# Phase tables in four operations, final states added once, and the layer norm of v on ScalarE and GpSimd

## The chip, the cores and the metric

The kernel runs on one core of a Trainium2 chip. The metric is the device time of one execution in microseconds (us). Before the change three executions took 1104.30, 1105.35 and 1107.51 us (median 1105.35). One more was profiled: it took 1104.05 us, and its span, from the first to the last instruction, is 1102.3 us.

## The reference

One decoder layer on 1024 prompt tokens and 64 sample tokens (8 sequences of 8), model width 1024, all in 32-bit floats:

```python
p = rmsnorm(x, norm1) @ w_in                       # 512 columns for S5, 512 u, 512 v
o_s5, hr, hi = s5_mixer(p[:, :512], h0, ...)       # 32 groups, 64 complex states each
u, v = gelu(p[:, 512:1024]), layernorm(gelu(p[:, 1024:]), ln_g, ln_b)
o_cm = u * (tril(W_s) @ v + b_s)                   # 8 heads, chunks of 128 positions
x = x + concat(rmsnorm(o_s5), rmsnorm(o_cm)) @ w_out
x = x + swiglu(rmsnorm(x), w_gate, w_up, w_down)
y = rmsnorm(x)
```

The S5 recurrence is `h[t] = a h[t-1] + B u[t]` with a complex diagonal `a`. The final states `hr`, `hi` and the rows of the normalised v in the last chunk are outputs too.

## The kernel before

**Stages.** The first is the norm and the S5 columns of the input projection (quarters 0 and 1 of `w_in`, `s5_in`, three token chunks of 384, 384 and 320). The second, from about 75 to 225 us, runs two things side by side: the S5 scan in eight parts of four groups (`s5_a`, `s5_b`, `s5_c`), and the gMLP branch: quarters 2 and 3 of the weights for v (`v_quarter`, nine blocks `j` of 128 tokens), the layer norm of each block (`ln`), then quarters 4 and 5 for u and the mixing (`cm_out`, a chunk at a time). Third comes the gated unit of S5 (`glu`), which reads all of the scan's output, then the output projection, and from about 360 us the feed-forward part, which fills two thirds of the span. Every large matmul is done three times (`mm3`, lines 150 to 152), for the high and low halves of its operands.

**Order.** The framework orders the instructions of each engine by a simulated timeline: it takes what is ready by its own costs, with the order of the code as the priority. Each engine then runs its list strictly in order, and so does the queue of transfers on SyncE (SP). The code of the S5 scan stands ahead of that of the gMLP branch; between them is no other order.

**Phase tables.** The scan is done in a rotating frame: 64 steps of cos and sin per group, split into a coarse and a fine table of eight entries, `tca, tsa` and `tcb, tsb`, made by doubling (lines 431 to 449: three levels each, six VectorE operations a level). For each part `s5_a` multiplies them out into `CO` and `SI` by six VectorE operations on 256 elements (lines 537 to 542), and ScalarE mirrors them (544) and copies the last column (545). `e64` holds that column.

**Final states.** `s5_a` computes the chunk sums by four matmuls in two PSUM banks, ScalarE copies 272 columns of each to `Ss` (510), and VectorE adds the last eight of each group to `fs` (511). Two transfers then swap the halves of `Ss` (513, 514).

**Layer norm of v.** `v_quarter(3, j)` ends with a GELU by ScalarE (650); `ln(j)` is then VectorE's statistics (654, 655), the addition of EPS (656), GpSimd's power of -0.5 (657), and the scaling on VectorE (658). Mixing (680) and the two outputs made on GpSimd (710, 711) read the result.

**Weights.** `load_q` brings half a quarter (512 KB) into a tile called `raw`, and ScalarE and VectorE split it into `cwr` (lines 146 and 147). There are three `raw` tiles for the whole kernel. Besides weights they hold masks and the two outputs of v. In the code the loads for quarter 4 (707) follow all of `ln`, and those for quarter 5 (715) follow the outputs of v.

Of the kernel before, what the change touches and what calls it, by code (L numbers as in the profile page):

```python
# [10 lines left out]
F32 = mybir.dt.float32  # L11
F32R = mybir.dt.float32r
I32 = mybir.dt.int32
AF = mybir.ActivationFunctionType
ALU = mybir.AluOpType
# [5 lines left out]
W = 512  # L21
NG = 32
# [6 lines left out]
EPS = 1e-6  # L29
# [54 lines left out]
def layer_kernel(ctx: ExitStack, tc: tile.TileContext, A, O, dbg=None):  # L84
# [133 lines left out]
    def pt(name, shape):  # L218
        return prep.tile([128] + list(shape), F32, tag=name, name=name)
# [111 lines left out]
    with tc.issue_after(GATE[GA].ins):  # L331
# [80 lines left out]
        fs = s5p.tile([128, NG, 9], F32, name="fs")  # L412
        t4, t5 = pt("e1", [NG, 8]), pt("t5", [NG])
# [11 lines left out]
        V.tensor_scalar(sn[:, 3:10, :], sn[:, 3:10, :], nsgn, None, op0=ALU.mult)  # L425

        e64 = s5p.tile([128, 2, NG], F32, name="e64")
        V.tensor_copy(e64[:, 0, :], co[:, 9, :])
        V.tensor_copy(e64[:, 1, :], sn[:, 9, :])
        tabs = {}  # L430
        for nm, lv, j0 in (("b", 3, 3), ("a", 3, 6)):
            n = 1 << lv
            tcn = s5p.tile([128, NG, n], F32, name=f"tc{nm}")
            tsn = s5p.tile([128, NG, n], F32, name=f"ts{nm}")
            V.memset(tcn[:, :, 0:1], 1.0)
            V.memset(tsn[:, :, 0:1], 0.0)
            for l in range(lv):
                m = 1 << l
                ec = co[:, j0 + l, :].unsqueeze(2).to_broadcast([128, NG, m])
                es = sn[:, j0 + l, :].unsqueeze(2).to_broadcast([128, NG, m])  # L440
                w1, w2 = pt("x1", [NG, 4])[:, :, :m], pt("e2", [NG, 4])[:, :, :m]
                V.tensor_tensor(w1, tcn[:, :, 0:m], ec, ALU.mult)
                V.tensor_tensor(w2, tsn[:, :, 0:m], es, ALU.mult)
                V.tensor_tensor(tcn[:, :, m:2 * m], w1, w2, ALU.subtract)
                w3, w4 = pt("e3", [NG, 4])[:, :, :m], pt("e4", [NG, 4])[:, :, :m]
                V.tensor_tensor(w3, tsn[:, :, 0:m], ec, ALU.mult)
                V.tensor_tensor(w4, tcn[:, :, 0:m], es, ALU.mult)
                V.tensor_tensor(tsn[:, :, m:2 * m], w3, w4, ALU.add)
            tabs[nm] = (tcn, tsn)
# [13 lines left out]
    BUFS = {"U": 2, "bc": 2, "T": 2, "Q": 2, "S": 2, "W": 2, "C": 2, "I": 2, "H": 2}  # L463
# [10 lines left out]
    def s5_a(pi):  # L474
# [31 lines left out]
        for h in range(2):  # L506
            sb = bank("sb", "s5")
            for g in range(2):
                PE.matmul(sb[:, 136 * g:136 * g + 136], Pg[:, 2 * h + g, :], U[:, 2 * h + g, :], start=True, stop=True)
            S.activation(Ss[:, 2 * h:2 * h + 2, :].rearrange("p g c -> p (g c)"), sb[:, 0:272], AF.Copy)  # L510
        V.tensor_tensor(fs[:, gs, 1:9], fs[:, gs, 1:9], Ss[:, :, 128:136], ALU.add)
# [14 lines left out]
        CO, SI = wt("C", "CO", (4, 128)), wt("I", "SI", (4, 128))  # L526
        t = wt("T2", "ct", (4, 8, 8))
        (tca, tsa), (tcb, tsb) = tabs["a"], tabs["b"]
        ch, sh = (x[:, :, 63:127].rearrange("p g (a b) -> p g a b", a=8) for x in (CO, SI))

        def oa(x):
            return x[:, gs, :].unsqueeze(3).to_broadcast([128, 4, 8, 8])

        def ob(x):
            return x[:, gs, :].unsqueeze(2).to_broadcast([128, 4, 8, 8])

        V.tensor_tensor(ch, oa(tca), ob(tcb), ALU.mult)
        V.tensor_tensor(t, oa(tsa), ob(tsb), ALU.mult)
        V.tensor_tensor(ch, ch, t, ALU.subtract)
        V.tensor_tensor(sh, oa(tsa), ob(tcb), ALU.mult)  # L540
        V.tensor_tensor(t, oa(tca), ob(tsb), ALU.mult)
        V.tensor_tensor(sh, sh, t, ALU.add)
        for i, x in enumerate((CO, SI)):
            S.activation(x[:, :, 0:63], x[:, :, 126:63:-1], AF.Copy, scale=(1.0, -1.0)[i])
            S.activation(x[:, :, 127:128], e64[:, i, gs].unsqueeze(2), AF.Copy)
# [46 lines left out]
    for pi in range(8):  # L592
        s5_b(pi)
        if pi < 7:
            s5_a(pi + 1)
        s5_c(pi)
    Q.dma_start(O["fs"], fs)
# [44 lines left out]
    st = lncp.tile([128, 9, 6], F32, name="st")  # L642
    mv = lncp.tile([128, 9, 2], F32, name="mv")

    def v_quarter(q, j):
        p = bank("pv")
        for k in range(8):
            wh, wl = wq(q, k, slice(0, 256))
            mm3(p[:, 0:256], xh[:, k, tok(j)], xl[:, k, tok(j)], wh, wl, k == 0, k == 7)
        S.activation(v[:, j, 256 * (q - 2):256 * (q - 1)], p[:, 0:256], AF.Gelu_apprx_tanh, scale=r1c[:, j:j + 1])  # L650

    def ln(j):
        vj = v[:, j, :]
        V.bn_stats(st[:, j, :], vj)
        V.bn_aggr(mv[:, j, :], st[:, j, :])
        V.tensor_scalar(mv[:, j, 1:2], mv[:, j, 1:2], EPS, None, op0=ALU.add)
        P.tensor_tensor(mv[:, j, 1:2], mv[:, j, 1:2], mhalf[:, 0:1], ALU.pow)
        V.tensor_scalar(vj, vj, mv[:, j, 0:1], mv[:, j, 1:2], op0=ALU.subtract, op1=ALU.mult)
# [165 lines left out]
    i = 0  # L824
# [515 lines left out]
```

## Time and profile before

| | |
|---|---|
| three executions, median | 1105.35 us |
| profiled execution, its time and its span | 1104.05 us, 1102.3 us |
| TensorE busy | 1049.9 us, 95% |
| VectorE busy | 852.9 us, 77% |
| ScalarE busy | 434.3 us, 39% |
| GpSimd busy | 320.5 us, 29% |
| mean granted clock of TensorE | 0.985 |

PE is TensorE (PEld its weight loads), DVE VectorE, ACT ScalarE, POOL GpSimd, and SPq the queue of transfers. A busy share is that of the whole span; what a stage is bound by shows in the windows of that stage, and in what each engine waited for. Durations of neighbouring instructions overlap by some tenths of a us, so the cost of one more in a full queue is the distance of two starts, a little less than its duration.

### The profile page before, as it was taken

The numbers are of one execution on the slowest core, as the hardware profiler recorded it, in microseconds if no ns is written. First come the engines' busy times: TensorE is split into PE (matmuls) and PEld (weight loads), VectorE is DVE, ScalarE is ACT, GpSimd is POOL, SyncE is SP. The second block draws the span as 40 slices with busy tenths as digits, with TensorE's granted clock in tenths as the row PEclk, the third lists the DMA queues.
The fourth block names the chain that finished last, engine by engine and source line by source line (L and its number), as shares of the span: only waits on it lengthen the run. The fifth ranks groups of instructions, "written<-read, shape, count | busy, mean of one in ns | idle before, by whom it ended". The sixth has DMA issues, their size and how long they took to land.

```text
span 1102.3 us, 20323 instructions
## 1 busy us (share of the span) xinstructions
PE 1049.9 (95%) x7966; PEld 1026.8 (93%) x7966; DVE 852.9 (77%) x1724; ACT 434.3 (39%) x812; POOL 320.5 (29%) x287
## 2 busy tenths in 40 slices
PE   7899999979999799999999999999998999999994
PEld 6899998879999699999999999999998999999994
DVE  6987999999998996666666666657668768758886
ACT  7314333487544543233233232233244325314651
POOL 5010350000000435425435334435433333223220
PEclk9989999989999899999999999999999999999998
DMA  8342334375332113223224223133156816514304
GB/s 278 108 129 65 89 99 124 90 225 164 113 113 95 39 58 129 77 90 129 75 76 137 82 77 128 59 110 127 61 181 219 303 40 205 184 35 151 119 16 162
DMA packets 81520, 131.19 MB, mean 119 GB/s; under 512 B 8977, under 2 KB 60049, under 8 KB 81297
## 3 DMA queue, kind: packets, MB, share of 16 engines
q1 hardware_dynamic: 81424, 129.91, 36.3%
q8 instruction: 62, 1.02, 0.4%
q14 instruction: 34, 0.27, 0.1%
HBM read 90.43 MB, written 34.24 MB: 113 GB/s over the span
## 4 chain that ended last, share of the span: by engine, by line
PE 50%; DVE 7%; DMA 5%; issue 2%; ACT 1%; POOL 0%; DVEq 0%; ACTq 0%; POOLq 0%; SPq 0%
PE u L152 12%; PE u L150 12%; PE u L151 12%; DMA h<-hid_d 4%; PE ua L152 3%; PE ua L151 2%; PE ua L150 2%; PE ub L151 1%; PE ub L152 1%; DVE xl L147 1%; PE ub L150 1%; ACT xh L146 1%; DVE fb L147 1%; PE uc L151 1%; PE uc L152 1%
## 5 line engine op out<-in xcount | busy, mean ns | idle before, releaser
L1059 POOL TENSOR_TENSOR tS<-q,q 128x512 f32<-128x512 f32 x22 | 28.6, 1301 | 251.7 <-DVE h L921 146.1
L150 PE MATMUL u<-xh,h 128*128 128x272 f32 x344 | 99.1, 288 | 0.0
L151 PE MATMUL u<-xl,h 128*128 128x272 f32 x344 | 99.0, 288 | 0.0
L152 PE MATMUL u<-xh,h 128*128 128x272 f32 x344 | 98.9, 288 | 0.0
L146 ACT ACTIVATE h<-q 128x512 fp32r<-128x512 f32 (+1 forms) x83 | 50.7, 614 | 81.7 <-PE u L151 56.8
L147 DVE TENSOR_TENSOR h<-q,h 128x512 fp32r<-128x512 f32 (+1 forms) x83 | 72.6, 876 | 4.3 <-ACT h L146 2.5
L150 PE MATMUL pu<-xh,cwr 128*128 128x384 f32 (+1 forms) x192 | 65.5, 345 | 6.2 <-DVE us L303 6.2
L1097 ACT ACTIVATE st<-st 128x272 f32<-128x272 f32 x88 | 37.8, 431 | 72.0 <-DVE st L1119 34.8
L152 PE MATMUL pu<-xh,cwr 128*128 128x384 f32 (+1 forms) x192 | 65.1, 342 | 0.0
L151 PEld LDWEIGHTS u<-xl,h 128*128 128x128 f32 x344 | 64.9, 189 | 0.0
L151 PE MATMUL pu<-xl,cwr 128*128 128x384 f32 (+1 forms) x192 | 64.8, 338 | 0.0
L150 PEld LDWEIGHTS u<-xh,h 128*128 128x128 f32 x344 | 64.7, 188 | 0.0
L152 PEld LDWEIGHTS u<-xh,h 128*128 128x128 f32 x344 | 64.6, 188 | 0.0
L1064 POOL TENSOR_TENSOR tS<-tS,q 128x512 f32<-128x512 f32 x22 | 30.0, 1363 | 111.3 <-DVE h L147 59.6
L146 ACT ACTIVATE fb<-q 128x512 fp32r<-128x512 f32 (+1 forms) x64 | 38.9, 609 | 58.3 <-PE u L151 35.8
L152 PE MATMUL u<-xh,fb 128*128 128x272 f32 x208 | 61.1, 294 | 0.6 <-DVE fb L147 0.6
L150 PE MATMUL u<-xh,fb 128*128 128x272 f32 x208 | 60.6, 291 | 0.1
L151 PE MATMUL u<-xl,fb 128*128 128x272 f32 x208 | 60.5, 291 | 0.0
L147 DVE TENSOR_TENSOR fb<-q,fb 128x512 fp32r<-128x512 f32 (+1 forms) x63 | 53.4, 850 | 5.3 <-ACT fb L146 4.4
L152 PE MATMUL po<-xh,cwr 128*128 128x272 f32 x192 | 55.9, 291 | 0.0
L151 PE MATMUL po<-xl,cwr 128*128 128x272 f32 x192 | 55.8, 290 | 0.0
L150 PE MATMUL po<-xh,cwr 128*128 128x272 f32 x192 | 55.5, 289 | 0.0
(498 smaller groups left out, 4122.8 us busy)
## 6 DMA issues: line engine op xcount, KB each, us to landing
hid_d<-st SPq DMA_DIRECT2D x22, 952.0 KB, 4.2
h<-hid_d SPq DMA_DIRECT2D x28, 544.0 KB, 4.0
q<-in_w_gate_dram SPq DMA_DIRECT2D x22, 512.0 KB, 3.5
q<-in_w_up_dram SPq DMA_DIRECT2D x22, 512.0 KB, 3.5
q<-in_w_d_dram SPq DMA_DIRECT2D x16, 512.0 KB, 3.7
wo<-in_w_out_dram SPq DMA_DIRECT2D x14, 512.0 KB, 4.9
wi<-in_w_in_dram SPq DMA_DIRECT2D x12, 512.0 KB, 5.1
h<-hid_d SPq DMA_DIRECT2D x14, 408.0 KB, 3.1
```

The costliest lines, as they stand in the source:

```text
L146: S.activation(hi, src, AF.Copy)
L147: return (eng or V).tensor_tensor(lo, src, hi.bitcast(F32), ALU.subtract)
L150: PE.matmul(p, wh, ah, start=start, stop=False, **kw)
L151: PE.matmul(p, wh, al, start=False, stop=False, **kw)
L152: return PE.matmul(p, wl, ah, start=False, stop=stop, **kw)
L1059: P.tensor_tensor(tS, a21, a22, ALU.add)
L1064: P.tensor_tensor(tS, tS, a11, ALU.subtract)
L1097: S.activation(dst, src, AF.Silu)
```

## The change

The fine table gets four entries at half steps (two levels in place of three, from the entries of `sn` and `co` one octave lower), the coarse one eight as before, started from the fine one's last entry. The tables are stored as pairs, so that sum and difference of two products give the forward and the backward half of each row: four VectorE operations a part. ScalarE makes the swapped copies once. The last eight columns are copied by ScalarE from PSUM to a tile `fsb`, and one addition after the last part puts them into `fs`. The layer norm takes its sum from the accumulator of the GELU, the sum of squares from a ScalarE pass that writes to a `raw` tile, five GpSimd operations on one column, and a ScalarE pass for the scaling.

```diff
-        V.tensor_scalar(sn[:, 3:10, :], sn[:, 3:10, :], nsgn, None, op0=ALU.mult)
+        V.tensor_scalar(sn[:, 2:10, :], sn[:, 2:10, :], nsgn, None, op0=ALU.mult)
...
+        tcb, tsb = (s5p.tile([128, NG, 2, 4], F32, name=n) for n in ("tcb", "tsb"))
+        ta1, ta2 = (s5p.tile([128, NG, 2, 8], F32, name=n) for n in ("ta1", "ta2"))
+        def powers(cs, ss, lv, j0):
...
+        V.tensor_copy(tcb[:, :, 0, 0], co[:, 2, :])
+        V.tensor_copy(tsb[:, :, 0, 0], sn[:, 2, :])
+        powers(tcb[:, :, 0, :], tsb[:, :, 0, :], 2, 3)
+        V.tensor_copy(ta1[:, :, 0, 0], tcb[:, :, 0, 3])
+        V.tensor_copy(ta1[:, :, 1, 0], tsb[:, :, 0, 3])
+        powers(ta1[:, :, 0, :], ta1[:, :, 1, :], 3, 6)
+        for x in (tcb, tsb):
+            S.activation(x[:, :, 1, :], x[:, :, 0, :], AF.Copy)
+        S.activation(ta2[:, :, 0, :], ta1[:, :, 1, :], AF.Copy)
+        S.activation(ta2[:, :, 1, :], ta1[:, :, 0, :], AF.Copy, scale=-1.0)
...
-            S.activation(Ss[:, 2 * h:2 * h + 2, :].rearrange("p g c -> p (g c)"), sb[:, 0:272], AF.Copy)
-        V.tensor_tensor(fs[:, gs, 1:9], fs[:, gs, 1:9], Ss[:, :, 128:136], ALU.add)
+            sb = sb[:, 0:272].rearrange("p (g c) -> p g c", g=2)
+            S.activation(Ss[:, 2 * h:2 * h + 2, 0:128], sb[:, :, 0:128], AF.Copy)
+            S.activation(fsb[:, g0 + 2 * h:g0 + 2 * h + 2, :], sb[:, :, 128:136], AF.Copy)
...
-        V.tensor_tensor(ch, oa(tca), ob(tcb), ALU.mult)
-        V.tensor_tensor(t, oa(tsa), ob(tsb), ALU.mult)
-        V.tensor_tensor(ch, ch, t, ALU.subtract)
-        V.tensor_tensor(sh, oa(tsa), ob(tcb), ALU.mult)
-        V.tensor_tensor(t, oa(tca), ob(tsb), ALU.mult)
-        V.tensor_tensor(sh, sh, t, ALU.add)
+        V.tensor_tensor(t1, oa(ta1), ob(tcb), ALU.mult)
+        V.tensor_tensor(t2, oa(ta2), ob(tsb), ALU.mult)
+        V.tensor_tensor(body[:, :, :, 4:8], t1, t2, ALU.subtract)
+        V.tensor_tensor(body[:, :, :, 3::-1], t1, t2, ALU.add)
         for i, x in enumerate((CO, SI)):
             S.activation(x[:, :, 0:63], x[:, :, 126:63:-1], AF.Copy, scale=(1.0, -1.0)[i])
-            S.activation(x[:, :, 127:128], e64[:, i, gs].unsqueeze(2), AF.Copy)
+        S.activation(CS[:, :, :, 127], e64[:, gs, :], AF.Copy)
...
+    V.tensor_tensor(fs[:, :, 1:9], fs[:, :, 1:9], fsb, ALU.add)
     Q.dma_start(O["fs"], fs)
...
-        S.activation(v[:, j, 256 * (q - 2):256 * (q - 1)], p[:, 0:256], AF.Gelu_apprx_tanh, scale=r1c[:, j:j + 1])
+        S.activation(v[:, j, 256 * (q - 2):256 * (q - 1)], p[:, 0:256], AF.Gelu_apprx_tanh, scale=r1c[:, j:j + 1],
+                     accum_out=st[:, j, q - 2:q - 1])
...
     def ln(j):
         vj = v[:, j, :]
-        V.bn_stats(st[:, j, :], vj)
-        V.bn_aggr(mv[:, j, :], st[:, j, :])
-        V.tensor_scalar(mv[:, j, 1:2], mv[:, j, 1:2], EPS, None, op0=ALU.add)
+        P.tensor_tensor(mv[:, j, 0:1], st[:, j, 0:1], st[:, j, 1:2], ALU.add)
+        P.tensor_scalar(mv[:, j, 0:1], mv[:, j, 0:1], -1.0 / W, None, op0=ALU.mult)
+        sq = raw("sqv", (W,))
+        S.activation(sq, vj, AF.Square, bias=mv[:, j, 0:1], accum_out=st[:, j, 2:3])
+        P.tensor_scalar(mv[:, j, 1:2], st[:, j, 2:3], 1.0 / W, EPS, op0=ALU.mult, op1=ALU.add)
         P.tensor_tensor(mv[:, j, 1:2], mv[:, j, 1:2], mhalf[:, 0:1], ALU.pow)
-        V.tensor_scalar(vj, vj, mv[:, j, 0:1], mv[:, j, 1:2], op0=ALU.subtract, op1=ALU.mult)
+        P.tensor_scalar(mv[:, j, 0:1], mv[:, j, 0:1], mv[:, j, 1:2], None, op0=ALU.mult)
+        S.activation(vj, vj, AF.Identity, scale=mv[:, j, 1:2], bias=mv[:, j, 0:1])
```

## Rows read from the trace of the kernel before

**Rows 1.** A wait of PE: engine, line, releaser, us in total, times, longest.
```profile
PE pu L150 <- DVE us L303: 6.2, 2, 5.2
```
**Rows 2.** Windows: us, then busy PE, PEld, DVE, ACT, POOL, granted clock, DMA share, GB/s.
```profile
55.50:61.50 6.00, 5.94 (x19) 5.97 (x20) 6.00 (x32) 0.00 (x0) 0.00 (x0) 0.50 0.00 1
110.00:155.00 45.00, 45.00 (x347) 43.35 (x346) 44.29 (x108) 15.52 (x36) 17.72 (x15) 1.00 0.31 84
75.00:225.00 150.00, 148.21 (x1141) 137.26 (x1139) 138.09 (x314) 57.77 (x130) 27.98 (x29) 1.00 0.37 101
231.10:235.40 4.30, 4.30 (x13) 4.30 (x14) 4.30 (x13) 4.30 (x14) 0.00 (x0) 0.50 1.13 361
```
**Rows 3.** Timeline around the first gated matmul; line 586: min/median/max ns, first and last start.
```profile
223.63 0.40 ACT L587 ACTIVATE ys<-yb 128x272 f32<-128x272 f32 x1 [0.29 <-PE yb L586]
224.51 4.10 SPq L757 DMA_DIRECT2D g<-ys_d  x4
231.10 2.61 PE L150 MATMUL pg<-xh,wgh 128*128 128x384 f32 x7 [6.01 <-ACT xh L770]
L586 PE MATMUL yb<-Hp,QK x64: 277/279/383, 111.3 to 223.3; 128*128 128x136 f32 x64
```
**Rows 4.** Timeline of DVE inside PE's wait at 50 us, first and last of six.
```profile
50.60 0.28 DVE L442 TENSOR_TENSOR x<-tcb,co 128x128 f32<-128x128 f32 x1
52.72 0.28 DVE L448 TENSOR_TENSOR tsb<-e,e 128x128 f32<-128x128 f32 x1
```
**Rows 5.** DVE by line, 0 to 260 us: count, busy us, mean ns, idle before.
```profile
L654 DVE BATCH_NORM_STATS2 st<-v 128x6 f32<-128x512 f32 x9 | 6.1, 676 | 0.0
L658 DVE TENSOR_SCALAR v<-v,mv 128x512 f32<-128x512 f32 x9 | 4.7, 525 | 0.0
L655 DVE BATCH_NORM_AGGREGATE mv<-st 128x2 f32<-128x6 f32 x9 | 1.4, 160 | 0.0
L656 DVE TENSOR_SCALAR mv<-mv 128x1 f32<-128x1 f32 x9 | 1.2, 129 | 0.0
L538 DVE TENSOR_TENSOR ct<-tsa,tsb 128x256 f32<-128x256 f32 x8 | 3.2, 406 | 0.0
L511 DVE TENSOR_TENSOR fs<-fs,Ss 128x32 f32<-128x32 f32 x8 | 2.5, 318 | 0.6 <-ACT Ss L510 0.6
```
**Rows 6.** ACT by line, 0 to 260 us.
```profile
L504 ACT ACTIVATE Pg<-ptr 128x512 f32<-128x512 f32 x8 | 4.7, 590 | 7.1 <-PE ptr L502 7.1
L510 ACT ACTIVATE Ss<-sb 128x272 f32<-128x272 f32 x16 | 6.2, 394 | 5.4 <-PE sb L509 3.6 <-issue 1.7
L545 ACT ACTIVATE CO<-e 128x4 f32<-128x4 f32 x8 | 1.6, 203 | 5.5 <-DVE gt L576 5.5
```
**Rows 7.** POOL: the power with min/median/max ns; a small operation by line.
```profile
L657 POOL TENSOR_TENSOR mv<-mv,mhalf x9: 541/1512/3400, 117.6 to 151.4; 128x1 f32<-128x1 f32 x9
L228 POOL TENSOR_SCALAR magt<-ld 128x32 f32<-128x32 f32 x1 | 0.3, 338 | 0.0
```
**Rows 8.** Loads of weights in the timeline of SPq and DVE, and the output of v.
```profile
78.26 0.34 SPq L242 DMA_DIRECT2D wi<-in_w_in_dram  x1
106.64 1.22 DVE L147 TENSOR_TENSOR cwr<-wi,cwr 128x1024 fp32r<-128x1024 f32 x1
155.25 0.43 SPq L242 DMA_DIRECT2D wi<-in_w_in_dram  x1
155.80 3.72 POOL L710 TENSOR_TENSOR cvs<-v,lgb 128x512 f32<-128x512 f32 x1 [2.53 <-DMA mb<-mb]
```
**Rows 9.** Where quarter 4 starts; the GELUs and the load's tile, min/median/max.
```profile
139.44 0.34 PE L150 MATMUL pu<-xh,cwr 128*128 128x384 f32 x1
L650 ACT ACTIVATE v<-pv,r1c x18: 456/474/481, 84.8 to 139.6; 128x256 f32<-128x256 f32 x18
L146 ACT ACTIVATE cwr<-wi x12: 1041/1052/1062, 8.0 to 178.4; 128x1024 fp32r<-128x1024 f32 x12
DMA to landing us min/median/max: 3.5/5.1/9.0
```

More of the change, by code (lines that the diff above doesn't have):

```diff
@@ L412, in layer_kernel @@
         fs = s5p.tile([128, NG, 9], F32, name="fs")
+        fsb = s5p.tile([128, NG, 8], F32, name="fsb")
         t4, t5 = pt("e1", [NG, 8]), pt("t5", [NG])
@@ L423, in layer_kernel @@
         Q.dma_start(dsk, A["dskip"])
-        V.tensor_scalar(sn[:, 3:10, :], sn[:, 3:10, :], nsgn, None, op0=ALU.mult)
[L427 to L436, printed above, removed]
+        V.tensor_scalar(sn[:, 2:10, :], sn[:, 2:10, :], nsgn, None, op0=ALU.mult)
+        e64 = s5p.tile([128, NG, 2], F32, name="e64")
+        V.tensor_copy(e64[:, :, 0], co[:, 9, :])
+        V.tensor_copy(e64[:, :, 1], sn[:, 9, :])
+        tcb, tsb = (s5p.tile([128, NG, 2, 4], F32, name=n) for n in ("tcb", "tsb"))
+        ta1, ta2 = (s5p.tile([128, NG, 2, 8], F32, name=n) for n in ("ta1", "ta2"))
+        def powers(cs, ss, lv, j0):
             for l in range(lv):
@@ L441, in layer_kernel @@
                 w1, w2 = pt("x1", [NG, 4])[:, :, :m], pt("e2", [NG, 4])[:, :, :m]
-                V.tensor_tensor(w1, tcn[:, :, 0:m], ec, ALU.mult)
-                V.tensor_tensor(w2, tsn[:, :, 0:m], es, ALU.mult)
-                V.tensor_tensor(tcn[:, :, m:2 * m], w1, w2, ALU.subtract)
+                V.tensor_tensor(w1, cs[:, :, 0:m], ec, ALU.mult)
+                V.tensor_tensor(w2, ss[:, :, 0:m], es, ALU.mult)
+                V.tensor_tensor(cs[:, :, m:2 * m], w1, w2, ALU.subtract)
                 w3, w4 = pt("e3", [NG, 4])[:, :, :m], pt("e4", [NG, 4])[:, :, :m]
[L446 to L449, printed above, removed]
+                V.tensor_tensor(w3, ss[:, :, 0:m], ec, ALU.mult)
+                V.tensor_tensor(w4, cs[:, :, 0:m], es, ALU.mult)
+                V.tensor_tensor(ss[:, :, m:2 * m], w3, w4, ALU.add)
+        V.tensor_copy(tcb[:, :, 0, 0], co[:, 2, :])
[8 more added lines that the diff above has]
+        S.activation(ta2[:, :, 1, :], ta1[:, :, 0, :], AF.Copy, scale=-1.0)
     prep_st.close()
@@ L461, in part @@
         return d[pi // 2].rearrange("t i g c -> (t i) (g c)")[:, 544 * (pi % 2):544 * (pi % 2) + 544]
-    BUFS = {"U": 2, "bc": 2, "T": 2, "Q": 2, "S": 2, "W": 2, "C": 2, "I": 2, "H": 2}
+    BUFS = {"U": 2, "bc": 2, "T": 2, "Q": 2, "S": 2, "W": 2, "C": 2, "H": 2}
     def wt(tag, name, shape):
@@ L525, in s5_a @@
             Q.dma_start(mb[16:32, :, 1:8, :], mb[0:16, :, 0:7, :])
[L526 to L529, printed above, removed]
+        CS = wt("C", "CS", (4, 2, 128))
+        CO, SI = CS[:, :, 0, :], CS[:, :, 1, :]
+        body = CS.rearrange("p g s c -> p (g s) c")[:, :, 63:127].rearrange("p x (a b) -> p x a b", a=8)
+        t1, t2 = wt("T2", "c1", (8, 8, 4)), wt("T3", "c2", (8, 8, 4))
         def oa(x):
-            return x[:, gs, :].unsqueeze(3).to_broadcast([128, 4, 8, 8])
+            return x[:, gs].rearrange("p g s a -> p (g s) a").unsqueeze(3).to_broadcast([128, 8, 8, 4])
         def ob(x):
-            return x[:, gs, :].unsqueeze(2).to_broadcast([128, 4, 8, 8])
-        V.tensor_tensor(ch, oa(tca), ob(tcb), ALU.mult)
-        V.tensor_tensor(t, oa(tsa), ob(tsb), ALU.mult)
-        V.tensor_tensor(ch, ch, t, ALU.subtract)
-        V.tensor_tensor(sh, oa(tsa), ob(tcb), ALU.mult)
-        V.tensor_tensor(t, oa(tca), ob(tsb), ALU.mult)
-        V.tensor_tensor(sh, sh, t, ALU.add)
+            return x[:, gs].rearrange("p g s b -> p (g s) b").unsqueeze(2).to_broadcast([128, 8, 8, 4])
+        V.tensor_tensor(t1, oa(ta1), ob(tcb), ALU.mult)
+        V.tensor_tensor(t2, oa(ta2), ob(tsb), ALU.mult)
+        V.tensor_tensor(body[:, :, :, 4:8], t1, t2, ALU.subtract)
+        V.tensor_tensor(body[:, :, :, 3::-1], t1, t2, ALU.add)
         for i, x in enumerate((CO, SI)):
             S.activation(x[:, :, 0:63], x[:, :, 126:63:-1], AF.Copy, scale=(1.0, -1.0)[i])
-            S.activation(x[:, :, 127:128], e64[:, i, gs].unsqueeze(2), AF.Copy)
+        S.activation(CS[:, :, :, 127], e64[:, gs, :], AF.Copy)
         S5[pi].update(QKf=QKf, Ss=Ss, Sw=Sw, CO=CO, SI=SI)
@@ L641, in layer_kernel @@
                                    op0=ALU.mult, op1=ALU.add)
-    st = lncp.tile([128, 9, 6], F32, name="st")
+    st = lncp.tile([128, 9, 3], F32, name="st")
     mv = lncp.tile([128, 9, 2], F32, name="mv")
```

## The prediction, made before the change was run

> **What bounds the kernel now.** I read the share of each engine first, then what PE waited for, then the windows of the stage that is changed. TensorE (PE) is busy for 95% of the span, so only work on the path to one of its few idle stretches can change the time. PE's waits have two long ones near the change. One of 5.2 us stands before the second chunk of the S5 input projection, behind the norm factors that VectorE makes [rows 1]. One of 6.0 us stands before the first matmul of the gated unit, which needs all of the scan's output [rows 3]. Both cost more than their length: the granted clock stands at 0.50, the lower of its two levels, for 6.0 us after the first and for 4.3 us after the second, where no matmul had run before [rows 2]; at half speed that is 3.0 and 2.15 us more.
>
> Between them, from 75 to 225 us, PE is busy for 148.2 of 150 us and VectorE for 138.1, ScalarE for 57.8, GpSimd for 28.0 [rows 2]. So PE and VectorE are both nearly full there, and in different ways: PE never starves, since the planner puts matmuls of the gMLP branch wherever the scan isn't ready, while the scan waits its turn on VectorE. At the end of the stretch both run out together. The scan's last output leaves ScalarE at about 224.0, its way through memory and back begins at 224.5 with the four loads, and PE starts again at 231.10 [rows 3]. From the last output to that start are 7.1 us, of which PE had other work for about one.
>
> **The change part by part.**
>
> *Making the tables.* The third level of the fine table goes: six operations of 0.28 us that stand between 50.6 and 53.0 us [rows 4], 0.2 us from start to start, 1.2 us in all. Four copies of one column take the place of four fills of the same size, about even. The six lie inside PE's wait for the norm factors, but the planner fills the gaps of that chain with whatever is ready, and the levels of the coarse table are next in line. I take nothing off that wait; between a gain of 1.2 and a loss of 1 us from another order. ScalarE's four copies (at most 0.6 us each, by the 512-element copy [rows 6]) find it idle there, 0.0 us busy from 55.5 to 61.5 [rows 2].
>
> *The tables of a part.* Two of six operations of 0.406 us go [rows 5]; with overlap 0.34 each, 0.67 us a part and 5.4 us over eight parts. The reversed write of the fourth is new; from no more to twice 0.41 us, and I take no more, as the same form of operands stands at 0.41 already.
>
> *Final states.* Eight additions of 0.32 us (0.1 us apart when nothing disturbs them) become one of 256 elements, 0.41 us; about 1 us less in all [rows 5]. ScalarE's evacuation of 272 columns, 0.39 us, becomes two; the small one costs like the copy of four columns, 0.2 us, less its overlap [rows 6]. That is sixteen times 0.1 to 0.2 us, less the eight copies of the last column that fall away. One small copy stands in the scan's chain ahead of the swap, 0.1 to 0.2 us a part, 1.6 us at most.
>
> *Layer norm.* VectorE loses 0.676, 0.160, 0.129 and 0.525 us per block [rows 5], 1.49 us, with overlap about 1.2, so 11 us over nine blocks. ScalarE gains two passes over 512 elements, 0.59 us by the nearest copy [rows 6]; bounds from no pointer operands to 0.8 us, I take 0.7. The reading of an accumulator by ScalarE is in no row: from nothing to 0.2 us (its smallest instruction), 27 of them; I take 0.1. Together 15 us, in a stretch where it is busy 15.5 of 45 us [rows 2], so it has room. GpSimd gets four small operations per block beside the power. By the nearest row they take 0.34 us [rows 7], 12 us in all, on 17.7 of 45 busy [rows 2].
>
> A rule speaks against this part: the Trainium skill (ScalarE: Activation LUTs, Rules for kernel authors) says to use VectorE, not ScalarE, for additions and products. By durations it is right here, as about 11 us of VectorE become 15 us of ScalarE and 12 of GpSimd. By that rule alone nothing would stand against the cost below, and the time would be about 1111. By occupancy [rows 2] the trace sides with the change: VectorE is the full one, and what is taken from it is worth more than what ScalarE pays.
>
> *What VectorE's relief is worth.* 11 + 5.4 + 1 is 17 us out of 138 in this stretch. PE's own list is as long as before, so nothing is won until the end, where the scan must finish earlier against PE's other work. It takes 6.2 us to close the wait at 225 us; I expect the scan to use at least that much of 17. Worth: 6.0 us idle and 2.15 us of low clock, 8.2 us.
>
> *What the scratch tile costs.* The squares go to a `raw` tile, of which there are three, and in the code nine such tiles now stand between the loads of quarter 3 and those of quarter 4. The trace shows how the three are handed out. Quarter 4's second half was loaded at 78.26 us, as soon as a tile was free. The next free tile came at about 107.9, when VectorE had finished its half of the split that began at 106.64. But quarter 5, next among the weights, was loaded only at 155.25, just as the second of the two outputs of v, which stand ahead of it in the code, was begun on GpSimd (155.80) [rows 8]. I read from this that tiles are handed out in the order of the code, each when its first writer is placed. Then quarter 4 cannot be loaded at 78; it follows the ninth block's pass of squares.
>
> In the trace before PE runs from quarter 3 straight into quarter 4 at 139.44, and the last GELU ends at 140.1 [rows 9]. In the changed kernel there follow two small GpSimd operations (0.7 us by [rows 7]), the issue of the load, its landing (3.5 to 5.1 us, I take 4.5), and ScalarE's half of the split, 1.05 us [rows 9]: the first matmul of quarter 4 can start at about 146.8, and the low half comes 1.2 us later [rows 8], of which about 0.9 shows. So PE has 7.4 + 0.9 = 8.3 us in which only the scan can feed it. The scan's last kind of matmul takes 64 x 0.28 us over eight parts [rows 3], 2.2 us a part, and its four other kinds (transposes, chunk sums, kernel, local outputs) I put at as much again: 4.4 us a part. The parts are 16 us apart (seven steps from 111.3 to 223.3), so over 8.3 us it fills 2.3, and up to 3 if it runs faster: 5.7 us idle remain. The low clock that followed the two waits above cost 2 to 3 us; here small matmuls fall into the gap, so from nothing to 3, and I take 1. Cost: 6.7 us. The load's two halves would find their cover, which was 60 us of lead, gone. SP's queue is no obstacle: the load stands between transfers of the scan, which don't wait for it.
>
> *Sum.* -8.2 for the gate of the gated unit, +6.7 for the late quarter 4, -0.5 for what else VectorE's relief does to short waits in this stretch: -2.0 us. Both are on PE's path, and the gap at 140 also gives the scan time, so the two can be added. Behind the gated unit no line is changed, and I take nothing there. Against the profiled execution that is 1104.05 - 2.0 = 1102.05; the median of the runs stands 1.3 us above it, so I predict 1103.3. Of this kernel a measurement can tell about 0.3%, 3.3 us, from no change.
>
> **The rivals.**
>
> *The load is not held back* (or the planner finds cover for it). Then the gate's gain stays whole: -8.2 to -10 us, 1096. For it: the order of handing out is read from one case, and SP's queue had other reasons to be late at 155 us. Against it: a tile stood idle for 47 us there.
>
> *GpSimd's chain delays quarter 4 further.* The power on one column took from 541 to 3400 ns [rows 7] while VectorE was busy. If each of the four small ones took 0.5 to 1 us in place of 0.34, a block would need 3.5 to 5.5 us with the median power. The GELUs, one per block and quarter, come every 3.2 us (18 from 84.8 to 139.6 [rows 9]), and that is the point from which it decides: above 3.2 us per block GpSimd falls behind. At 4 us the ninth block is 7 us late, which adds 7 us to the gap at 140: 1110.5, and I put the case at 1111. Against it: the planner's picture of GpSimd was near the truth before, as the scaling on VectorE never waited for the power (0.0 us idle before it [rows 5]). The Trainium skill (GPSIMD Engine Reference, Specifications) names a cause, SBUF interfaces shared with VectorE, contended by operations with two SBUF inputs. That is what VectorE mostly runs here, and the spread of the power agrees, though no row separates it.
>
> *The scan does not use the relief.* The planner, not a rule of the kernel, decides what VectorE does in freed time. If it spends it on work of the gMLP branch, the scan gains on PE only what the gap at 140 gives it; of the 8.2 us at the gate then 3 to 6 are won, and the time is 1105.5 to 1108.5. The 2 to 3 us of scan work that fill that gap speak against it.
>
> **How the numbers follow.** Forecast (both effects, near balance) 0.48; load not held back 0.27; GpSimd's chain longer 0.15; relief unused 0.10. Inside the forecast its terms move by 3 us either way, so about a fifth of it comes out faster than 3.3 us and a tenth slower. Faster: 0.27 + 0.09 = 0.36. Slower: 0.13 + 0.05 = 0.18. Same: 0.46. The forecast's own range is 1100 to 1107; the range reaches to the first rival and to the near end of the second, 1095 to 1110.
>
> **What would show it.** In the changed trace: no wait of PE before the first gated matmul, or one under 1 us; the last GELU of the scan at least 7 us before it; VectorE busy for about 120 us between 75 and 225 us; the loads of quarter 4 at 140 to 143 us in SP's queue, and an idle PE before line 150's first `pu` of quarter 4, released by ScalarE's or VectorE's split; GpSimd's small operations at 0.25 to 0.5 us. I am wrong if quarter 4 is loaded before 110 us (first rival), if GpSimd's operations of a block take over 4 us (second), or if the wait before the gated unit stays (third).

## The result: 1.3% slower, and the profile after

The changed kernel took 1118.55 us in the median of three executions (1118.42, 1118.55 and 1122.21) against 1104.8 us of the kernel before, measured beside it. A fourth execution took 1467 us at a mean clock of 0.65 and is left out. The ratio is 1.0128, with a 95% interval of 1.0107 to 1.0148, so 12 to 16 us lost. The forecast was 1103.3 us, and the range ended at 1110. The profiled execution took 1118.55 us, and its span is 1116.4 us, 14.1 more than before.

PE is still the busy engine. The first part of the profile, of the kernel after (engine, busy us, share, instructions):

```profile
PE 1056.5 (95%) x7966; PEld 1029.8 (92%) x7966; DVE 836.6 (75%) x1659; ACT 447.3 (40%) x868; POOL 337.4 (30%) x323
```

The list of what PE waited for, in the kernel after (engine, line, releaser: us in total, times, longest):

```profile
PE sb L519 <- ACT Pg L514: 11.3, 2, 7.6
PE pu L150 <- DVE us L303: 6.9, 2, 5.1
...
PE po L150 <- DVE x1q L863: 3.3, 1, 3.3
...
PE pu L150 <- ACT cwr L146: 1.8, 1, 1.8
```

The second line answers to [rows 1] and is near what it was. The 6.0 us before the first matmul of the gated unit [rows 3] are gone, as forecast. New is the first line: the scan's chunk sums (`sb`) wait for ScalarE's copy of the transposed table (`Pg`), once for 7.64 us and once for 3.65 us. A wait of 3.3 us for `x1q` (the input, loaded again for the sum with the output projection), behind the gated unit, is new too, and so is the last line, the wait for the late quarter 4: 1.8 us. The windows that answer to [rows 2], two of 25 us and one of 7.6 us, of the kernel after (us; busy PE, PEld, DVE, ACT, POOL; granted clock; DMA share; GB/s):

```profile
110.00:155.00 45.00, 33.72 (x258) 31.89 (x257) 26.75 (x59) 20.06 (x57) 27.02 (x36) 0.88 0.30 82
75.00:225.00 150.00, 136.89 (x1027) 127.21 (x1025) 114.20 (x234) 66.10 (x176) 45.06 (x65) 0.95 0.39 110
...
125.00:150.00 25.00, 17.28 (x122) 15.86 (x120) 15.19 (x32) 11.03 (x31) 15.89 (x20) 0.80 0.23 63
150.00:175.00 25.00, 19.61 (x135) 17.09 (x136) 17.68 (x28) 14.99 (x39) 16.03 (x27) 0.93 0.46 138
...
121.35:128.96 7.61, 6.67 (x57) 6.47 (x55) 7.58 (x19) 0.00 (x0) 7.61 (x1) 1.00 0.16 43
```

And the two of 25 us in the kernel before:

```profile
125.00:150.00 25.00, 25.00 (x190) 24.16 (x189) 24.46 (x61) 7.79 (x18) 10.57 (x8) 1.00 0.27 74
150.00:175.00 25.00, 24.80 (x186) 22.25 (x185) 24.97 (x48) 9.73 (x22) 11.21 (x9) 1.00 0.59 173
```

From 110 to 155 us PE was busy for all 45 us before; now it is for 33.7, at a mean clock of 0.88. VectorE fell from 44.3 to 26.8 us. Most of that isn't relief: it stood still for 9.65 us from 129.59 us on, and for 5.62 us before 155.57 us. Between 125 and 175 us PE is idle for 13.1 us (50 less 17.28 and 19.61; 0.2 before), and its mean clock is 0.80 and 0.93 in the two halves. The waits for `Pg` and for quarter 4 are these 13.1 us (11.3 and 1.8). That is where the loss arises.

How it comes about is read in the timeline. In the kernel after, around the longest wait (start us, us, engine, line, operation, tiles; in brackets the idle time before it and what ended it):

```profile
120.82 0.22 DVE L534 TENSOR_TENSOR mb<-mb,dk 16x64 f32<-16x64 f32 x1 [0.82 <-ACT mb L530]
120.96 0.67 DVE L587 TENSOR_TENSOR Hp<-gt,gw 128x508 f32<-128x508 f32 x1
...
121.35 7.61 POOL L671 TENSOR_SCALAR mv<-mv 128x1 f32<-128x1 f32 x1
...
128.07 0.72 DVE L507 TENSOR_TENSOR QK<-QK,qkt 128x576 f32<-128x576 f32 x1
128.83 0.76 DVE L506 TENSOR_TENSOR qkt<-bc,psn 128x576 f32<-128x576 f32 x1
...
128.99 0.81 ACT L672 ACTIVATE v<-v,mv 128x512 f32<-128x512 f32 x1 [8.10 <-POOL mv L671]
...
135.01 0.59 ACT L514 ACTIVATE Pg<-ptr 128x512 f32<-128x512 f32 x1
...
135.66 2.18 PE L519 MATMUL sb<-U,Pg 128*128 128x136 f32 x8 [7.64 <-ACT Pg L514]
```

A product of one column on GpSimd, 0.3 us in most blocks, lasts 7.61 us. In that time, the last of the windows of the kernel after, ScalarE does nothing at all. VectorE runs two-input operations without a gap: each starts some 0.07 us before the one ahead has ended. Its row has its first gap, 0.04 us, from 128.79 to 128.83, and GpSimd's operation ends at 128.96. It reads only what GpSimd itself had written, so it wasn't waiting for data. ScalarE stands in its own order at the scaling of the norm for 8.10 us, and behind it stand the gelus, the scan's outputs and `Pg`. PE then runs out of work. Five GpSimd instructions per block, in the kernel after (min/median/max ns, first and last start):

```profile
L665 POOL TENSOR_TENSOR mv<-st x9: 192/342/6153, 113.0 to 162.8; 128x1 f32<-128x1 f32 x9
L666 POOL TENSOR_SCALAR mv<-mv x9: 207/228/719, 115.6 to 163.2; 128x1 f32<-128x1 f32 x9
L669 POOL TENSOR_SCALAR mv<-st x9: 190/190/1008, 116.8 to 164.5; 128x1 f32<-128x1 f32 x9
L670 POOL TENSOR_TENSOR mv<-mv,mhalf x9: 567/577/1122, 117.2 to 166.8; 128x1 f32<-128x1 f32 x9
L671 POOL TENSOR_SCALAR mv<-mv x9: 295/296/7610, 117.9 to 168.8; 128x1 f32<-128x1 f32 x9
```

The medians of the four small ones, 0.19 to 0.34 us, agree with the 0.34 us that the prediction took [rows 7]. Two of 45 instructions, those of 7.61 and 6.15 us, hold 13.8 of the 33.6 us that the 45 take. Behind the first ScalarE waits 8.10 us, behind the second 6.47 us, each time with `Pg` further back in its queue, and PE's two waits for `Pg` follow. The maximum is what to look at here; the median doesn't show it.

### The profile page after: what moved, and what is told of

It is laid out like the page before. It is cut to its first block, busy times and chain, and to the rows that moved or that the text cites. A ratio compares the mean times of both kernels' runs of the same rounds, so it can differ in the third digit from the quotient of the medians.

```text
span 1116.4 us, 20364 instructions
## 1 busy us (share of the span) xinstructions
PE 1056.5 (95%) x7966; PEld 1029.8 (92%) x7966; DVE 836.6 (75%) x1659; ACT 447.3 (40%) x868; POOL 337.4 (30%) x323
## 4 chain that ended last, share of the span: by engine, by line
PE 72%; DVE 11%; DMA 7%; POOL 3%; ACT 3%; issue 3%; SPq 0%; DVEq 0%; ACTq 0%; POOLq 0%
PE u L151 12%; PE u L150 12%; PE u L152 12%; DMA h<-hid_d 4%; PE ua L151 3%; PE ua L152 3%; PE ua L150 3%; PE po L150 3%; PE po L151 2%; PE po L152 2%; PE pu L150 2%; PE pu L152 2%; PE pu L151 2%; DVE xl L147 1%; PE ub L151 1%
```

## Experiments

Three theories stood at the start. A: the load of quarter 4 comes late, since it must wait for the squares' tiles, and PE waits for it. B: GpSimd's one-column operations don't get on while VectorE runs two-input operations without a gap, and ScalarE, the scan and PE wait in turn. C: ScalarE's 18 more passes, between the scan's copies, cost by themselves. Ratios are to the kernel before, measured beside each run; one per cent is 11 us.

**The tables alone** (the changed kernel, with the layer norm of before):

```diff
-        P.tensor_tensor(mv[:, j, 0:1], st[:, j, 0:1], st[:, j, 1:2], ALU.add)
...
-        S.activation(vj, vj, AF.Identity, scale=mv[:, j, 1:2], bias=mv[:, j, 0:1])
+        V.bn_stats(st[:, j, :], vj)
...
+        V.tensor_scalar(vj, vj, mv[:, j, 0:1], mv[:, j, 1:2], op0=ALU.subtract, op1=ALU.mult)
```

> The tables and the final states of the change, with the layer norm of before (VectorE's statistics, one power on GpSimd). All theories put the loss into the layer norm, so none of the new waits of PE between 120 and 170 us should be there. VectorE is relieved by about 6 us of 138 between 75 and 225 us: if the scan uses it, the wait before the gated unit falls from 6.0 us to 0 to 3 us and the time to 1098 to 1103; if the planner spends it elsewhere, 1103 to 1107. Quarter 4 loaded before 85 us.

Measured: 1106.97 us, ratio 0.9996 (0.9980 to 1.0013), so no difference. The wait before the gated unit fell as expected, and the time did not follow. The first matmul of the gated unit starts at 225.7 us in place of 231.1, with only 0.5 us of waiting before it. But the last matmul of the output projection starts at 359.1 against 357.1. The 5.4 us gained at the gate are gone behind it, in these lines of PE's waits in the run with the tables alone:

```profile
PE po L150 <- DVE x1q L859: 5.0, 1, 5.0
...
PE po L150 <- ACT xh L146: 1.0, 1, 1.0
```

**The layer norm alone** (the kernel before, with the new norm; the inverse edit).

> The kernel before with the new layer norm alone. If the loss is that of the layer norm (late quarter 4, or GpSimd held up by VectorE): 1112 to 1125, with GpSimd operations on one column of over 5 us and PE waiting for a ScalarE evacuation of the scan. If the tables had a part in the loss: under 1110.

Measured: 1126.69 us, ratio 1.0179 (1.0155 to 1.0202), a little above the range expected. The loss is the norm's. Three waits for `Pg` in this run:

```profile
PE sb L509 <- ACT Pg L504: 14.8, 3, 5.7
```

Three one-column operations of GpSimd last 6.35, 6.88 and 7.49 us here, on three different lines (655, 659 and 656), so it isn't one operation's kind. At the end of each VectorE had run out of work; it then stood idle for 5.9 to 8.8 us.

**A scratch of its own for the squares** (the changed kernel):

```diff
-        sq = raw("sqv", (W,))
+        sq = cwf[:, 0:W]
```

> The changed kernel with the squares written to a stretch of cwf that is idle then, in place of a raw tile; all else equal. Theory A (the late load of quarter 4 is what costs): quarter 4 is loaded before 85 us, PE's waits between 120 and 170 us nearly go, 1096 to 1104. Theory B (GpSimd's one-column operations cannot run beside back-to-back VectorE operations with two inputs, ScalarE waits for them, the scan's evacuations stand behind it): quarter 4 is early, but operations of 5 to 8 us on GpSimd and PE's wait for Pg remain in kind, 1110 to 1120.

Measured: 1123.04 us, ratio 1.0142 (1.0119 to 1.0166): nothing gained, and 3 us above theory B's range. Quarter 4 is loaded early again, and the wait for `Pg` is longer. The timeline of SyncE's queue in this run:

```profile
78.02 0.34 SPq L242 DMA_DIRECT2D wi<-in_w_in_dram  x1
```

And PE's waits in it:

```profile
PE sb L519 <- ACT Pg L514: 13.9, 4, 5.0
```

So the late load isn't what the changed kernel loses by, though it is late there (both halves from 160.68 us on).

**The four small operations on VectorE** (the changed kernel, scratch from the `raw` tiles; only the power stays on GpSimd):

```diff
-        P.tensor_tensor(mv[:, j, 0:1], st[:, j, 0:1], st[:, j, 1:2], ALU.add)
+        V.tensor_tensor(mv[:, j, 0:1], st[:, j, 0:1], st[:, j, 1:2], ALU.add)
...
```

> The changed kernel with the four small operations of each block on VectorE, only the power left on GpSimd as before; the squares still go to a raw tile. Theory A: quarter 4 is loaded late as in the change, 1112 to 1120. Theory B: ScalarE waits for VectorE's 0.1 us operations in place of GpSimd's; PE's wait for Pg (11.3 us) goes, quarter 4 is loaded at 140 to 148 us instead of 160.7, last v matmul at 138 to 145 us instead of 160.5; a wait for quarter 4 of 4 to 8 us as first predicted; 1099 to 1107.

Measured: 1112.85 us, ratio 1.0043 (1.0026 to 1.0060). By the time alone that is theory A's range and not theory B's. But more than half of the loss is gone, and so is every wait for `Pg`. What is left has another place, in the rows of this run:

```profile
164.03 6.03 POOL L725 TENSOR_TENSOR cvs<-cvs,lgb 128x512 f32<-128x512 f32 x1
...
170.08 0.55 SPq L726 DMA_DIRECT2D out_cvs_dram<-cvs  x1
...
173.41 0.38 SPq L489 DMA_DIRECT2D U<-us_d  x1
...
182.09 2.15 PE L519 MATMUL sb<-U,Pg 128*128 128x136 f32 x8 [6.29 <-DMA U<-us_d]
```

The sum for v's second output takes GpSimd 6.03 us (2.5 us in the kernel before, on line 711). SyncE's queue stands behind that output's transfer from 162.4 to 170.1 us. The scan's load of `U` comes after it, and PE waits 6.29 us for it.

**Both together** (the four small operations on VectorE, and the own scratch).

> After with both suspects taken out: the norm's four one-column operations of arithmetic on VectorE (only the power stays on GpSimd), and the scratch of the squares a tile of its own, so that quarter 4's loads need not wait. Theory B (GpSimd starved, with the late loads only coming out once that is gone): quarter 4's loads are issued near 75 to 79 us as before, PE waits for no Pg and for no U of more than 2 us, time 1098 to 1105 us, 6 to 15 us under the kernel with the small operations on VectorE alone. Theory C (ScalarE's 18 more passes between the scan's copies cost by themselves): 1109 us or more, with PE waiting for ScalarE before the gated unit.

Measured: 1104.37 us, ratio 0.9975 (0.9958 to 0.9991): theory B's number, and the end of theory C. ScalarE does the norm's 18 passes here too, and PE never waits for `Pg`. Against the run with the own scratch alone this one differs only in the engine of four one-column operations, and it is 18.5 us by the ratios (1.0142 less 0.9975, times 1107). Against the run with the small operations alone on VectorE the own scratch brings 7.5 us, as if the late load cost that much; the last pair of runs points to another cause.

**GpSimd's hold-up by itself: a queue of small operations nobody needs** (the kernel before, six after each block of quarter 2):

```diff
...
+        if q == 2:
+            for i in range(6):
+                P.tensor_scalar(zz[:, j, i:i + 1], v[:, j, i:i + 1], 2.0, None, op0=ALU.mult)
```

> Before with 54 more one-column GpSimd operations (six after each block of quarter 2, results unused, nobody waits for them). Theory B (a GpSimd operation does not get on while VectorE runs two-input operations without a gap): some of the 54 last several us in the stretch from 85 to 95 us, in which VectorE has no gap, the others 0.2 to 0.6 us; time within 0.3% of before, since nobody waits. Rival (the long ones of after only show GpSimd waiting for ScalarE's results): none of the 54 is over 2 us, since each has its input long before it starts.

Measured: 1106.75 us, ratio 1.0000 (0.9985 to 1.0015), and of the 54 operations, in this run's group by line:

```profile
L655 POOL TENSOR_SCALAR zz<-v x54: 201/321/1225, 84.5 to 104.3; 128x1 f32<-128x1 f32 x54
```

Theory B failed on its own terms. VectorE had no gap from 84.8 to 93.6 us, and yet none of the 54 took over 1.23 us. The rival's number came out, but its reason, that GpSimd only waits for ScalarE, doesn't fit the operation of 7.61 us above.

**ScalarE waits for nobody** (the changed kernel; mean square less squared mean, five small operations and the scaling on VectorE, power on GpSimd, own scratch):

```diff
-        S.activation(sq, vj, AF.Square, bias=mv[:, j, 0:1], accum_out=st[:, j, 2:3])
+        S.activation(sq, vj, AF.Square, accum_out=st[:, j, 2:3])
...
-        S.activation(vj, vj, AF.Identity, scale=mv[:, j, 1:2], bias=mv[:, j, 0:1])
+        V.tensor_scalar(vj, vj, mv[:, j, 0:1], mv[:, j, 1:2], op0=ALU.subtract, op1=ALU.mult)
```

> After with a norm in which ScalarE waits for nobody: the squares without the mean straight after the gelu, five one-column operations on VectorE, the power on GpSimd, and the last scaling on VectorE as before; the variance is then the mean square less the squared mean. Theory B: no starvation on ScalarE's queue, PE waits for no Pg; VectorE gets less relief (0.525 us a block more than with the scaling on ScalarE), time 1098 to 1106 us. Theory C: like before or slower, 1106 to 1112 us.

Measured: 1104.54 us, ratio 0.9988 (0.9967 to 1.0008). Neither the waits of ScalarE that are left in the run with both nor VectorE's extra scaling show in the time.

**The new norm without the new tables** (the kernel before, new norm, four small operations on VectorE, own scratch).

> Before with the new norm, its small operations on VectorE and a scratch of its own, without the four-operation tables. If the tables are worth nothing by themselves (their run alone was within 0.2% of before), it comes within 3 us of the same kernel with the tables; if they matter once VectorE carries the small operations, it is 4 us or more slower than that.

Measured: 1106.94 us, ratio 1.0002 (0.9987 to 1.0017). By the ratios the tables are worth 3 us beside the mended norm, at the edge of what was called nothing; the two intervals overlap, so that isn't shown.

**Lone operations on GpSimd** (the kernel before; two after each block of quarters 2 and 3, the second reading the first, so that GpSimd goes idle between blocks; their results aren't used):

```diff
...
+        i = 2 * (q - 2)
+        P.tensor_scalar(zz[:, j, i:i + 1], v[:, j, 256 * (q - 2):256 * (q - 2) + 1], 2.0, None, op0=ALU.mult)
+        P.tensor_scalar(zz[:, j, i + 1:i + 2], zz[:, j, i:i + 1], 2.0, None, op0=ALU.mult)
```

> Before with two one-column GpSimd operations after each block of quarters 2 and 3 (the second reads the first's result; nobody needs them), so that GpSimd goes idle between blocks and most come to it while VectorE is in the middle of a gapless stretch. In the queue of 54 none was over 1.23 us; of these 36, theory B2 (an operation that comes to an idle GpSimd in the middle of a gapless stretch of VectorE gets in only where that stretch ends, while a queue already running gets its share) expects several in the stretch from 86 to 95 us to last until about 93.6 us, 2 us or more. Rival B3 (no such stretch holds GpSimd up; what was long in after has another cause, in the norm's own operands): all under 1.3 us.

Measured: 1109.91 us in a single execution (before, beside it: 1107.31, from 1101.94 to 1109.08), and in this run's timeline:

```profile
85.04 0.69 DVE L491 TENSOR_TENSOR PT<-bc,wr 128x512 f32<-128x512 f32 x1 [1.43 <-DMA bc<-in_bc_dram]
85.09 0.72 POOL L655 TENSOR_SCALAR zz<-zz 128x1 f32<-128x1 f32 x1
...
90.41 0.54 POOL L654 TENSOR_SCALAR zz<-v 128x1 f32<-128x1 f32 x1 [1.06 <-ACT v L652]
...
117.86 1.97 POOL L654 TENSOR_SCALAR zz<-v 128x1 f32<-128x1 f32 x1 [4.06 <-ACT v L652]
...
119.69 0.67 DVE L659 BATCH_NORM_STATS2 st<-v 128x6 f32<-128x512 f32 x1
...
126.35 2.23 POOL L654 TENSOR_SCALAR zz<-v 128x1 f32<-128x1 f32 x1
```

Both theories fail in part. The operation at 90.41 comes to an idle GpSimd in the middle of the gapless stretch and takes 0.54 us, against B2. The same line with the same operands takes 1.97 and 2.23 us later, without the norm's operands, against B3. The one of 1.97 us ends at 119.83 with no gap of VectorE near, just behind the start of a VectorE operation with one input. So what VectorE does at the time decides.

One thing sets the two kinds of stretch apart in all the traces: a VectorE operation on 16 partitions (16x64: `mb<-mb,dk` or `dk<-idn,dsk`) earlier in the same gapless stretch, as at 120.82 in the kernel after. Between 75 and 225 us, 127 one-column GpSimd operations, the powers apart, start while VectorE is busy. With no such operation ahead of them stand 95, and the longest takes 1.36 us; behind one stand 32, among them all 17 that take over 1.4 us. The powers and GpSimd's 128x512 operations don't sort as cleanly (a power of 3.02 us started with none ahead). No run moves that operation, so this is a coincidence of rows and not a shown cause.

**The scaling back on VectorE** (the changed kernel with its own scratch, the small operations on GpSimd):

```diff
-        S.activation(vj, vj, AF.Identity, scale=mv[:, j, 1:2], bias=mv[:, j, 0:1])
+        V.tensor_scalar(vj, vj, mv[:, j, 1:2], mv[:, j, 0:1], op0=ALU.mult, op1=ALU.add)
```

> After with its own scratch, where the small operations stay on GpSimd but the last scaling goes back to VectorE, which then waits for GpSimd in its own order. Its twin with the scaling on ScalarE was 1123.0 us. Theory B: VectorE's gapless stretches now end at the latest at the scaling that waits for GpSimd, so one-column operations of over 4 us become fewer, Pg is held up less, and the time falls to 1106 to 1116 us. Rival (the loss comes from the chain ScalarE - GpSimd - ScalarE as such, however long GpSimd takes): 1118 us or more.

Measured: 1119.99 us, ratio 1.0131 (1.0092 to 1.0169), the rival's number, but the rows don't bear the rival out. In this run:

```profile
138.53 4.42 POOL L665 TENSOR_TENSOR mv<-st 128x1 f32<-128x1 f32 x1 [0.70 <-ACT v L660]
...
145.45 0.55 DVE L672 TENSOR_SCALAR v<-v,mv 128x512 f32<-128x512 f32 x1 [2.57 <-POOL mv L671]
...
162.07 6.07 POOL L725 TENSOR_TENSOR cvs<-cvs,lgb 128x512 f32<-128x512 f32 x1
...
177.16 0.79 PE L594 MATMUL yb<-U,mb 128*128 128x136 f32 x2 [7.46 <-DMA mb<-mb]
```

VectorE comes to the scaling and stands there for GpSimd, and then the operation of 4.42 us (138.53 to 142.95) gets through: VectorE's idle time of 2.57 us begins at 142.88. None of the one-column operations is longer than 4.42 us, and PE's waits for `Pg` shrink to one of 1.03 us. But v's second output takes 6.07 us on GpSimd again, and the wait that comes of it, 7.46 us, takes the place of what was won. This run can't tell the two apart by its time.

**The products of v's outputs on VectorE**, in the run with the small operations on VectorE and in that with both:

```diff
-        P.tensor_tensor(t, v[:, j, :], lng, ALU.mult)
-        P.tensor_tensor(t, t, lnb, ALU.add)
+        V.tensor_tensor(t, v[:, j, :], lng, ALU.mult)
+        V.tensor_tensor(t, t, lnb, ALU.add)
```

> The kernel with the small operations on VectorE (scratch still from the raw tiles, 1112.85 us), with the two products and two sums of the v outputs also moved from GpSimd to VectorE (four operations of 128x512, about 2.7 us of VectorE at 0.67 us each). There one of them took 6.03 us on GpSimd, SyncE stood behind the output's transfer from 162 to 170 us, and PE then waited 6.3 us for U. If that (GpSimd's second hold-up) made up most of the 7.5 us to the kernel with its own scratch: 1103 to 1107 us and no wait for U over 2 us. If the raw tile handed out late makes them up: 1108 us or more.

> The same move in the kernel with its own scratch (1104.37 us), where those operations took 1.3 to 4.6 us on GpSimd and SyncE did not stand long behind them. Theory: GpSimd's hold-up no longer sets anything there, and VectorE pays 2.7 us more: within 3 us of it, 1102 to 1107 us. If GpSimd's delays still matter: 1100 us or less.

Measured: with the scratch from the `raw` tiles 1104.49 us, ratio 0.9982 (0.9964 to 1.0000); with the own scratch 1104.33 us, ratio 0.9977 (0.9957 to 0.9996). By the ratios the first falls 7 us under its twin, as the theory of GpSimd's second hold-up has it; the second stays where it was. With GpSimd out of the way the late load costs nothing that can be measured: 0.2 us between the two, where each interval is about 2 us either way. It is still late, as SyncE's queue shows in the first run:

```profile
148.63 0.93 SPq L242 DMA_DIRECT2D wi<-in_w_in_dram  x2
```

The windows of that run:

```profile
125.00:150.00 25.00, 23.14 (x199) 21.33 (x197) 22.39 (x68) 17.31 (x50) 5.31 (x10) 1.00 0.42 111
150.00:175.00 25.00, 21.98 (x149) 20.76 (x150) 25.00 (x52) 10.27 (x23) 4.04 (x5) 1.00 0.65 191
```

The same windows of the run with the early load, and the one behind the gate:

```profile
125.00:150.00 25.00, 25.00 (x197) 24.05 (x196) 22.43 (x67) 17.20 (x47) 8.79 (x10) 1.00 0.40 106
150.00:175.00 25.00, 25.00 (x180) 22.56 (x179) 24.77 (x54) 11.08 (x29) 3.09 (x5) 1.00 0.59 184
...
250.00:275.00 25.00, 19.99 (x136) 18.73 (x135) 23.12 (x62) 11.67 (x24) 0.00 (x0) 0.93 0.52 168
```

PE idles 4.9 us more between 125 and 175 us with the late load. With the early load it idles 5.0 us behind the gate, for `x1q` (3.0 us) and for ScalarE's split of the gated output (2.0 us). The first of these, in the run with the early load:

```profile
264.31 1.03 DVE L147 TENSOR_TENSOR xl<-v,xh 128x256 fp32r<-128x256 f32 x4
...
265.37 5.89 SPq L849 DMA_DIRECT2D x1q<-in_xT_dram  x8
...
272.83 0.39 PE L150 MATMUL po<-xh,fb 128*128 128x272 f32 x1 [3.00 <-DVE x1q L863]
```

The load of `x1q` starts when VectorE has read v for the last time. That is at 265.4 us, while the kernel before, with a gate 9.0 us later, starts it at 265.0. So this load comes no earlier for the earlier gate. How the gain at the gate fades, by the first start of the gated unit's matmuls and the last start of the output projection's, both from the tiles' groups in each profile, in us:

| kernel | first of the gated unit | last of the output projection |
|---|---|---|
| before | 231.1 | 357.1 |
| tables alone | 225.7 | 359.1 |
| both undone | 226.9 | 357.9 |
| products on VectorE, late load | 227.6 | 358.0 |
| products on VectorE, early load | 222.1 | 354.6 |
| after | 241.5 | 371.0 |

A gate that opens 3.5 to 9 us earlier brings the start of the output projection's last matmul from 2.0 us later to 2.5 us earlier. These are single profiled executions.

## Why the prediction was wrong, step by step

**The step that failed is the price of GpSimd's small operations.** "By the nearest row they take 0.34 us [rows 7], 12 us in all" priced them by one row from another stage, and the wait of ScalarE for them at nothing. The nine powers, with 541 to 3400 ns, stood in the same stretch and in the same group of rows, and showed that one column can cost six times its shortest there. In the changed kernel the same kind of instruction cost up to 7.61 us. The prediction also did not ask what is queued behind the waiting instruction on ScalarE: the gelus, the scan's outputs and `Pg`. PE's waits for `Pg`, 11.3 us, stand in no term of its sum. By the runs that price is 18.5 us with the own scratch. In the changed kernel itself, the small operations and then v's outputs off GpSimd take it from 1.0128 to 1.0043 to 0.9982, 9.4 and 6.8 us.

**The rival on GpSimd's chain** named the right mechanism, a GpSimd held up by VectorE, and had 0.15 of the chance. Its form was wrong. It had all blocks 0.5 to 1 us per operation slower, with 3.2 us a block as the point from which it decides, and charged the delay to quarter 4's load. In fact most blocks ran as priced, one operation took 2.59 us and two took over 6 us, and PE lost by ScalarE's queue; its wait for quarter 4 was 1.8 us. The sign given for this rival, over 4 us of GpSimd in a block, came true in two blocks. The argument against the rival, that the scaling on VectorE "never waited for the power", was read wrongly. With 0.0 us idle before it VectorE had other work; that says nothing on how late the power was.

**What is known of the hold-up.** Shown: the same operations on VectorE cost nothing that can be measured, and on GpSimd 18.5 us. In the rows of the norm's runs, long operations end where VectorE's gapless stretch does (128.96 against 128.79, and 142.95 against 142.88 in the run with the scaling back on VectorE). The Trainium skill (SBUF — State Buffer, Who interferes with whom) says that a VectorE instruction with two SBUF inputs contends with a GpSimd instruction that reads SBUF. It also says (the same page, SBUF: two separate sides) that whoever of the two starts first holds the shared ports for the whole instruction. The rows agree on who contends. On how long they agree only where the operations are short: the one that starts at 85.09 in the run with lone operations ends at 85.81, less than 0.1 us behind the VectorE operation that ran when it came. In the kernel after 7.61 us span the 19 VectorE instructions of that window, not one. That VectorE then hands over only at a gap or at an operation with one input is read from these rows and tested by no run, and why one stretch holds GpSimd up and another doesn't stays open; the 16x64 operation ahead is the one difference found.

**The gate.** "Worth: 6.0 us idle and 2.15 us of low clock" held as far as the gate. ScalarE's copy of the scan's last output starts at 219.1 us in place of 223.63, PE waits for nothing before the first gated matmul, and no low clock follows. In the changed kernel that proves little, since PE came to the gate late by itself: the last `pu` matmul starts 19.6 us later than before (238.4 against 218.8), the first of the gated unit 10.4, so 9.2 us came back there. The relief of the scan is shown by the run with both undone, where that copy starts at 209.4. What failed is "Behind the gated unit no line is changed, and I take nothing there". An earlier gate runs into `x1q`, whose load starts only when VectorE is through with v, and of 5.4 us at the gate (the tables alone) nothing was left at the end of the output projection, of 9.0 us (products on VectorE, early load) 2.5.

**The late quarter 4.** The mechanism was read rightly: tiles are handed out in the order of the code, and the load waits for the ninth block's squares, at 148.6 us in the run with the products on VectorE (140 to 143 forecast) and at 160.7 in the changed kernel. PE's idle time was sized well in that run, 4.9 us against 5.7; in the changed kernel, where the waits for `Pg` came first, it was 1.8. Of the price of 6.7 us nothing can be measured (0.2 us). So the two terms could not simply be added: between the late and the early load 5.5 us at the gate become 3.4 at the end of the output projection, since the waits behind the gate take up a part. Where the rest goes was not followed.

**The small terms.** Rows of the kernel after, by line (count; busy us, mean ns; idle before):

```profile
L672 ACT ACTIVATE v<-v,mv 128x512 f32<-128x512 f32 x9 | 7.3, 814 | 15.6 <-POOL mv L671 15.6
...
L668 ACT ACTIVATE sqv<-v,mv 128x512 f32<-128x512 f32 x9 | 6.5, 720 | 12.0 <-POOL mv L666 12.0
...
L660 ACT ACTIVATION_READ_ACCUMULATOR v<-pv,r1c 128x1 f32 x18 | 3.5, 196 | 0.0
```

The reading of an accumulator is an instruction of its own, 0.19 us, the upper bound and not the 0.1 taken. The two passes take 0.72 and 0.81 us where 0.7 was taken. ScalarE's small evacuation (0.18 us) and the one addition (0.42 us) cost what was said. The tables' reversed write costs nothing over the plain form (lines 548 to 551 have means of 409 to 422 ns), and the making of the tables left PE's wait where it was (5.2 before, 5.1 after). None of these shows in the time of the run with both undone, which has them all.

**The kernel that came out ahead** is the changed one with the four small operations on VectorE and the own scratch: 0.9975 (0.9958 to 0.9991), some 17 us under the changed kernel and about 3 under the one before, which is at the edge of what was said to be no change. The products moved as well add nothing that can be measured.

## What to carry to other kernels

When work goes to an engine that shares something with a busy one, price it by the longest row of its kind in that very stretch, and name everything that stands behind the instruction that will wait for it. One-column operations in a chain between two in-order engines belong on an engine that isn't held up there, here VectorE, even if it is the fuller one: 36 of them on VectorE cost nothing measurable here, on GpSimd 9 to 18 us. And before a wait's length is booked as a gain, look for what is late next: here 5 to 9 us at a gate were worth 0 to 3 behind it.

## What the runs showed of the hardware that was not expected

A one-column GpSimd operation of 0.2 to 0.3 us lasted up to 7.61 us beside a VectorE running 128x512 and 128x576 two-input operations, and one of 128x512 lasted 6.03 to 6.07 us where 1.3 us is its shortest. VectorE's own operations next to it kept their 0.67 to 0.76 us. In another stretch with the same kinds of VectorE operations, without a gap for almost 9 us, at most 0.72 us was enough. All one-column operations over 1.4 us between 75 and 225 us, the powers apart, had a VectorE operation on 16 partitions ahead of them in the same gapless stretch; whether that is the cause was not tested. In the norm's runs the stall ended itself: VectorE ran dry because ScalarE was stuck, ScalarE because GpSimd was, and GpSimd got through when VectorE had nothing left, or one operation of 0.76 us.
